# Two-layer mixer trunk on one core: the last output stage's final products five steps later, and the start of layer B reordered

## The chip, the core and the metric

The program runs on one core of a Trainium2 chip. The metric is the device time of one execution in microseconds (us); the number given for a kernel is the median over its runs. The engines are named as in the profile: PE (TensorE, the matrix products), DVE (VectorE), ACT (ScalarE), POOL (GpSimd) and SP (SyncE, which here only issues transfers). Each engine works through its own queue in order.

## The reference

The input x is 2048 positions by 1024 channels in float32. Two layers follow, each of the form x <- x + mixer(RMSNorm(x)), and then a last RMSNorm:

```
h = rmsnorm(x, norm_g[0]);  x = x + recurrent_mixer(h, ...)     # layer A
h = rmsnorm(x, norm_g[1]);  x = x + shortconv_mixer(h, ...)     # layer B
out = rmsnorm(x, final_g)
```

`rmsnorm` multiplies each position by the reciprocal root of the mean of its squares over the 1024 channels, and by a gain per channel. Layer A projects h to 2 x 1536 channels, runs a convolution, gates and a linear recurrence over the positions, and projects back to 1024. Layer B projects h to 4 x 1536 channels, forms products, a short convolution and a SiLU gate, and projects back.

## The kernel before

All tensors lie transposed, channels on the 128 partitions and positions along the row. The 2048 positions are four chunks `c` of 512, which form two halves of two chunks; 1024 channels are eight blocks `d` of 128. A float32 product is made of three float16 products (`mm3`, lines 500, 503 and 504): each operand is split into a high and a low float16 part, the high part by an ACT cast and the low part by a DVE subtraction (`add`, lines 311 and 313; weights in `split`, lines 420 and 421; the last stage's operands in `split_out`, lines 1117 and 1118).

The work has four stages: projection into layer A, projection out of A (`OutProj`, with `emitA` and `endA`), projection into B (`in_B`, made of units), projection out of B (`OutSums`, with `emitB`, `endB` and `last_chunk`). The two stages around the change are these.

**Layer B's beginning.** The products of B's projection use seven combinations of operand blocks in the manner of Strassen and Winograd. A unit is seven steps of 12 matmuls. `build_h` (line 329) makes the operands of h for one half: it normalises x blocks (`normed`, line 305, DVE), forms the sums and differences T1 to T4 (T1 at line 351, T3 at 367 and T4 at 371 on POOL; T2 at 357 on DVE), and splits B11, T1, T2, B21, B22, T3, T4 in this order, one of these groups of four per call. For the first half it runs beside the last products of A's output projection, in two parts (`besideA`, line 1603). For the second half it runs in `second_half` (line 1647), a side list that is advanced by one call after each product step of the units. There, chunk 2 is already normalised (`ready`), while the norm of chunk 3 has to wait for A's last output block: its squares are summed block by block into the tile `sa` (`add_square`, the addition on POOL, line 230), summed over the partitions by PE (`sums_of`, line 236, tile `ss`), and turned into `inv` by `inv_from` (line 244): root on ACT, reciprocal on DVE, four diagonal tiles `dg` on DVE (line 259), a PE product that spreads them (line 262, tile `pn`), a copy on ACT (line 265). `inv_between` (line 292) issues the two PE parts in two calls and places each behind the product that was last issued then (`pe_last`). The calls of the list are: first the four B11 splits, second the `ss` sums, third the inverse, fourth T1, and so on. An eviction of a product from its accumulator is at line 539 (DVE) or at 549 and 565 (ACT).

**Layer B's output projection.** `OutSums.run` makes seven products of four blocks `q` per half, again in combinations: a step is one accumulator of 18 matmuls. Each finished accumulator (`acc`, six buffers) is evicted by `add_to_x` (line 1428, DVE) one step after it was filled (`lag(1)`). After each step `tick` counts the deferred calls down. The final values of chunk 1 are complete with the sixth combination of the first half, those of chunk 0 four steps later, with the seventh. `endB` (line 1690) then defers the end of the chunk, a generator `ended`: for chunks 0 and 1 `inv_between` with POOL as queue sums by PE, takes the root and reciprocal, and issues two transfers from POOL: `r` to memory (line 252, `rd<-r`) and back, spread over the partitions (line 253, `inv<-rd`), the second waiting for the first. The next call multiplies the eight blocks by `inv` (line 1701, six on DVE, two on POOL) and stores them from SP (line 1702). The calls come four, five and six steps after the end of the chunk is reported; for chunk 2 they come after two, three and four. Chunk 3 ends in `last_chunk`.

The order of the instructions on each engine follows from the program's order, from priorities (evictions come first) and from the scheduler's own timing model, which is not the chip's.

Of the kernel before, what the change touches and what calls it, by code (L numbers as in the profile page):

```python
# [11 lines left out]
ALU = mybir.AluOpType  # L12
# [9 lines left out]
KB = D // P  # L22
# [24 lines left out]
def trunk(ctx, tc, xT, xn, prm, wa, ga, oa, wb, ob, out):  # L47
    nc = tc.nc
    v, s, g, sp = nc.vector, nc.scalar, nc.gpsimd, nc.sync
# [48 lines left out]
    def pair16(pool, tag, name, bufs):  # L98
        t = pool.tile([P, 2, ROW], F16, tag=tag, name=name, bufs=bufs)
        return t[:, :, 0:CH]  # L100
# [94 lines left out]
    def et(name, dt=F32):  # L195
        return buf(wk, "e", name, NE, dt)
# [16 lines left out]
    def xt(name, dt=F32):  # L213
        return buf(opp, "x", name, 36, dt)
# [10 lines left out]
    def add_square(acc, x, first, eng):  # L225
        if first:
            return s.activation(acc, x, AF.Square)
        sq = et("sq")[:, 0 : x.shape[1]]
        ins = s.activation(sq, x, AF.Square)
        squared[0] = eng.tensor_tensor(out=acc, in0=acc, in1=sq, op=ALU.add)  # L230
        return ins

    def sums_of(acc, ss, behind=None):

        for i in range(acc.shape[1] // P):
            ins = nc.tensor.matmul(  # L236
                ss[:, i : i + 1], acc[:, i * P : (i + 1) * P], ones[:, 0:1],
                start=True, stop=True,
            )
            if behind is not None:  # L240
                after(ins, behind)
        return ins

    def inv_from(ss, inv, queue, copy, behind=None):

        n = inv.shape[1] // P
        r = cst.tile([P, 4], F32, tag="r", name="r", bufs=2)[:, 0:n]
        s.activation(r, ss, AF.Sqrt, bias=epst[:, 0:1], scale=1.0 / D)
        v.reciprocal(r, r)
        if queue:  # L250
            rd = dr.tile([CH], F32, tag="rd", name="rd", bufs=2)
            queue.dma_start(rd.rearrange("(i p) -> p i", p=P), r)
            queue.dma_start(inv, rd.partition_broadcast(P))
            return
        pn = ps.tile([P, CH], F32, tag="g", name="pn", bufs=2)[:, 0 : n * P]
        dgs = buf(wk, "dg", "dg", 2)
        for i in range(n):
            dg = dgs[:, i * P : (i + 1) * P]
            v.tensor_scalar(
                out=dg, in0=col(PC_ID, P), scalar1=r[:, i : i + 1], scalar2=None, op0=ALU.mult  # L260
            )
            ins = nc.tensor.matmul(pn[:, i * P : (i + 1) * P], ones, dg, start=True, stop=True)  # L262
            if behind is not None:
                after(ins, behind)
        copy(inv, pn)
        return ins
# [25 lines left out]
    def inv_between(acc, inv, queue=None):  # L292

        ss = ps.tile([P, 4], F32, tag="g", name="ss", bufs=2)[:, 0 : acc.shape[1] // P]
        with tc.high_priority(PR):
            sums_of(acc, ss, pe_last[0])
        if not queue:
            yield
        with tc.high_priority(PR):
            inv_from(ss, inv, queue, s.copy, pe_last[0])  # L300
        yield


    def normed(l, x, kk, inv):
        return v.scalar_tensor_tensor(
            out=x, in0=x, scalar=gs[l][:, kk : kk + 1], in1=inv, op0=ALU.mult, op1=ALU.mult
        )

    def add(ops, name, k, src):
        t = pair16(opp, "op", "op", NOP)  # L310
        hi = s.activation(t[:, 0, :], src, AF.Copy)  # L311
        ops[name, k] = t
        return hi, v.tensor_tensor(out=t[:, 1, :], in0=src, in1=t[:, 0, :], op=ALU.subtract)  # L313
# [15 lines left out]
    def build_h(l, x, inv, ks, ops, ready=()):  # L329

        def norm(kk, c):
            if c not in ready:
                ins = normed(l, x[kk, c], kk, inv[c])
                if evac_last[0] is not None:
                    after(ins, evac_last[0])

        def block(name, k, kk, c):
            if (name, k) not in ops:  # L340
                norm(kk, c)
                add(ops, name, k, x[kk, c])

        t1, t2 = {}, {}
        for k in ks:
            block("B11", k, k, 0)
        yield
        for k in ks:
            norm(k, 1)
            t1[k] = et("t1")  # L350
            g.tensor_tensor(out=t1[k], in0=x[k, 1], in1=x[k, 0], op=ALU.subtract)
            add(ops, "T1", k, t1[k])
        yield
        for k in ks:
            norm(k + 4, 1)
            t2[k] = et("t2")
            v.tensor_tensor(out=t2[k], in0=x[k + 4, 1], in1=t1[k], op=ALU.subtract)
            add(ops, "T2", k, t2[k])
        yield
        for k in ks:  # L360
            block("B21", k, k + 4, 0)
        yield
        for k in ks:
            add(ops, "B22", k, x[k + 4, 1])
        yield
        for k in ks:
            g.tensor_tensor(out=x[k, 1], in0=x[k + 4, 1], in1=x[k, 1], op=ALU.subtract)
            add(ops, "T3", k, x[k, 1])
        yield
        for k in ks:  # L370
            g.tensor_tensor(out=t2[k], in0=x[k + 4, 0], in1=t2[k], op=ALU.subtract)
            add(ops, "T4", k, t2[k])
        yield

# [266 lines left out]
    def defer(fn, steps):  # L641
        deferred.append([steps, fn])
# [440 lines left out]
    def after(ins, first):  # L1083
        tc.add_manual_dep(
            ins.ins, first.ins.name,
            mybir.DependencyInfo(mybir.DependencyClass.NoSync, mybir.DependencyReason.SCHED_ONLY),
            reason="order",
        )
# [491 lines left out]
    hB, inv, sums, w0 = [{}, {}], {}, {}, {}  # L1580
    early, sws, xB, xh = [], [], {}, {}

    def emitA(c, d, xr, acc, undo):
        evac_last[0] = v.scalar_tensor_tensor(
            out=xr, in0=acc, scalar=undo, in1=xr, op0=ALU.mult, op1=ALU.add
        )
        sp.dma_start(x2[c][d * P : (d + 1) * P, :], xr)
        first = c not in sums
        if first:
            sums[c] = et("sa")  # L1590
            if c % 2 == 0:
                inv[c // 2] = [xt("inv") for i in range(2)]
        add_square(sums[c], xr, first, g)

    def endA(c):
        if c == 3:
# [41 lines left out]

    stay = [(d, c) for c in range(4) for d in range(KB) if c > 1]
    outA.run(emitA, endA, besideA, sideA, {dc: kept_x(*dc) for dc in stay})  # L1640
    x = {(d, c): xB[d, 2 + c] for d in range(KB) for c in range(2)}
    while early:
        run(early.pop(0))
    w0 = w0, ahead(1, wb[1], sws[1])
    acc3 = sums[3]

    def second_half():
        h = build_h(1, x, inv[1], range(4), hB[1], (0,))
        next(h)
        yield  # L1650
        yield from inv_between(acc3, inv[1][1])
        yield from h

    sideB = [second_half()]


# [33 lines left out]
    def endB(c, ts):  # L1690
        if ts is not CHUNK:
            defer(lambda: endings.append(last_chunk(c, ts)), 1 if ts is FIRST else 0)
            return
        iv = et("inv")

        def ended():
            yield from inv_between(sums[c], iv, g if c < 2 else None)
            for d in range(KB):
                f = kept[c, d]
                eng = g if d % 3 == 2 else v  # L1700
                eng.tensor_tensor(out=f, in0=f, in1=iv, op=ALU.mult)  # L1701
                sp.dma_start(out[d * P : (d + 1) * P, c * CH : (c + 1) * CH], f)

        steps = ended()
        for n in range(3):
            defer(lambda: next(steps, None), (4 if c < 2 else 2) + n)


    POOLED = (5, 7)
# [66 lines left out]

    ending = end_of_all()
    outB.run(emitB, endB, ending)
    tick(KB)
    while next(ending) != "idle":  # L1780
# [72 lines left out]
```

## Time and profile before

| | us |
|---|---|
| median of 3 runs | 2008.2 |
| lowest and highest run | 2005.45 and 2008.68 |
| the profiled execution's own time | 2011.81 |
| its span, first to last instruction | 2010.0 |
| PE busy | 1963.9 |
| DVE busy | 1259.9 |
| ACT busy | 1001.8 |
| POOL busy | 641.9 |

Busy time counts the stretches in which an engine has an instruction in work. The span lies 1.8 us below the time of the same execution. A number such as L1701 is a line of the kernel; `op<-t,op` reads "writes op, from t and op"; an arrow before a releaser says what ended the idle time.

### The profile page before, as it was taken

The numbers are of one execution on the slowest core, as the hardware profiler recorded it, in microseconds if no ns is written. First come the engines' busy times: TensorE is split into PE (matmuls) and PEld (weight loads), VectorE is DVE, ScalarE is ACT, GpSimd is POOL, SyncE is SP. The second block draws the span as 40 slices with busy tenths as digits, with TensorE's granted clock in tenths as the row PEclk, the third lists the DMA queues.
The fourth block names the chain that finished last, engine by engine and source line by source line (L and its number), as shares of the span: only waits on it lengthen the run. The fifth ranks groups of instructions, "written<-read, shape, count | busy, mean of one in ns | idle before, by whom it ended". The sixth has DMA issues, their size and how long they took to land. (4 is left out here: it accounts for less than half of the span.)

```text
span 2010.0 us, 25206 instructions
## 1 busy us (share of the span) xinstructions
PE 1963.9 (98%) x9064; PEld 916.0 (46%) x9064; DVE 1259.9 (63%) x2112; ACT 1001.8 (50%) x1816; POOL 641.9 (32%) x511
## 2 busy tenths in 40 slices
PE   8999999999999999998999999999999999999978
PEld 3444444444444444443444444444444444444436
DVE  7977666667574745479546757748547448654455
ACT  7878786868483623145443343343432432435332
POOL 0001010101010313365553583664644534512221
PEclk9999999999999999999999999999999999999989
DMA  9111313052104714421140251242220120595442
GB/s 311 49 63 50 102 38 113 24 168 83 65 17 157 248 66 162 95 79 63 63 152 32 79 163 43 95 142 79 74 100 22 53 90 21 194 378 200 134 152 85
DMA packets 130958, 216.25 MB, mean 108 GB/s; under 512 B 13200, under 2 KB 41488, under 8 KB 130832
## 3 DMA queue, kind: packets, MB, share of 16 engines
q1 hardware_dynamic: 130384, 213.58, 31.9%
q8 instruction: 71, 1.16, 0.3%
q0 software_dynamic: 448, 1.06, 0.2%
q14 instruction: 55, 0.45, 0.1%
HBM read 152.19 MB, written 62.40 MB: 107 GB/s over the span
## 5 line engine op out<-in xcount | busy, mean ns | idle before, releaser
L503 PEld LDWEIGHTS <-wc 128*128 128x128 f16 x2096 | 205.3, 98 | 271.1 <-issue 37.6
L500 PEld LDWEIGHTS <-wc 128*128 128x128 f16 x2096 | 207.9, 99 | 254.1 <-issue 19.6
L504 PEld LDWEIGHTS <-wc 128*128 128x128 f16 x2096 | 205.6, 98 | 257.3 <-issue 15.8
L503 PE MATMUL acc<-op,wc 128*128 128x512 f16 x752 | 285.3, 380 | 2.8 <-DVE op L313 2.8
L504 PE MATMUL acc<-op,wc 128*128 128x512 f16 x752 | 285.7, 380 | 0.0
L500 PE MATMUL acc<-op,wc 128*128 128x512 f16 x752 | 283.3, 380 | 1.3 <-ACT op L311 1.3
L903 POOL TENSOR_TENSOR u<-fixed,u 128x512 f32<-128x512 f32 x48 | 51.3, 1090 | 557.0 <-ACT fixed L900 557.0
L500 PE MATMUL q<-op,wc 128*128 128x512 f16 x576 | 217.4, 380 | 9.8 <-DVE pb L539 4.0
L503 PE MATMUL q<-op,wc 128*128 128x512 f16 x576 | 219.0, 380 | 0.0
L504 PE MATMUL q<-op,wc 128*128 128x512 f16 x576 | 218.5, 380 | 0.0
L421 DVE SCALAR_TENSOR_TENSOR wc<-ws,fixed,wc 128x512 f16<-128x512 f32 x104 | 104.4, 1008 | 90.5 <-ACT wc L420 81.0
L500 PE MATMUL p<-op,wc 128*128 128x512 f16 x384 | 146.1, 381 | 2.7 <-DVE pb L539 2.7
L500 PE MATMUL acc<-op,wf 128*128 128x512 f16 (+1 forms) x384 | 136.3, 355 | 11.1 <-DVE xo L1428 11.1
L503 PE MATMUL p<-op,wc 128*128 128x512 f16 x384 | 146.3, 381 | 0.0
L504 PE MATMUL p<-op,wc 128*128 128x512 f16 x384 | 146.2, 381 | 0.0
L500 PE MATMUL acc<-zs,wf 128*128 128x512 f16 x384 | 145.5, 379 | 0.0
L503 PE MATMUL acc<-zs,wf 128*128 128x512 f16 x384 | 145.5, 379 | 0.0
L504 PE MATMUL r<-op,wc 128*128 128x512 f16 x384 | 145.5, 379 | 0.0
L503 PE MATMUL r<-op,wc 128*128 128x512 f16 x384 | 145.5, 379 | 0.0
L500 PE MATMUL r<-op,wc 128*128 128x512 f16 x384 | 145.5, 379 | 0.0
L504 PE MATMUL acc<-zs,wf 128*128 128x512 f16 x384 | 145.2, 379 | 0.0
L504 PE MATMUL acc<-op,wf 128*128 128x512 f16 (+1 forms) x384 | 136.3, 355 | 0.0
(197 smaller groups left out, 3544.1 us busy)
## 6 DMA issues: line engine op xcount, KB each, us to landing
wr<-in_wb SPq DMA_DIRECT2D x104, 256.0 KB, 3.5
xs<-in_xT SPq DMA_DIRECT2D x48, 256.0 KB, 5.4
z<-sg SPq DMA_DIRECT2D x48, 256.0 KB, 2.0
zr<-z SPq DMA_DIRECT2D x48, 256.0 KB, 5.2
zr<-zT SPq DMA_DIRECT2D x48, 256.0 KB, 5.3
wr<-in_wa SPq DMA_DIRECT2D x44, 256.0 KB, 4.2
zB<-ed SPq DMA_DIRECT2D x36, 256.0 KB, 2.0
zT<-cg SPq DMA_DIRECT2D x36, 256.0 KB, 2.0
```

What stands on the lines that cost most here:

```text
L421: v.scalar_tensor_tensor(out=t[:, 1, :], in0=src, scalar=sw[:, 2:3], in1=t[:, 0, :], op0=ALU.mult, op1=ALU.subtract,)
L500: ins = nc.tensor.matmul(acc, wh, xh, start=start, stop=False, **kw)
L503: nc.tensor.matmul(acc, wh, xl, start=False, stop=False, **kw)
L504: return nc.tensor.matmul(acc, wl, xh, start=False, stop=stop, **kw)
L903: g.tensor_tensor(out=u, in0=w, in1=u, op=ALU.mult)
```

## The change

Three edits. First, T1, T3 and T4 in `build_h` (both halves) are computed by DVE rather than POOL, and so is the last addition of squares of layer A's output, that of block 7 of chunk 3. Second, `second_half` issues the `ss` sums in its first call, with the four B11 splits and now the four B21 splits as well; the inverse in its second call; T1 in its third. Third, for chunks 0 and 1 of the last stage the products with `inv` come nine steps after the report of the chunk's end, not five; the sums still come after four. Chunk 2 keeps its steps.

```diff
@@ build_h
-            g.tensor_tensor(out=t1[k], in0=x[k, 1], in1=x[k, 0], op=ALU.subtract)
+            v.tensor_tensor(out=t1[k], in0=x[k, 1], in1=x[k, 0], op=ALU.subtract)
...
-            g.tensor_tensor(out=x[k, 1], in0=x[k + 4, 1], in1=x[k, 1], op=ALU.subtract)
+            v.tensor_tensor(out=x[k, 1], in0=x[k + 4, 1], in1=x[k, 1], op=ALU.subtract)
...
-            g.tensor_tensor(out=t2[k], in0=x[k + 4, 0], in1=t2[k], op=ALU.subtract)
+            v.tensor_tensor(out=t2[k], in0=x[k + 4, 0], in1=t2[k], op=ALU.subtract)
@@ emitA
-        add_square(sums[c], xr, first, g)
+        add_square(sums[c], xr, first, v if (c, d) == (3, KB - 1) else g)
@@ second_half
         h = build_h(1, x, inv[1], range(4), hB[1], (0,))
+        steps = inv_between(acc3, inv[1][1])
+        next(steps)
         next(h)
-        yield
-        yield from inv_between(acc3, inv[1][1])
+        for k in range(4):
+            add(hB[1], "B21", k, x[k + 4, 0])
+        yield
+        next(steps)
+        yield
         yield from h
@@ endB
-        for n in range(3):
-            defer(lambda: next(steps, None), (4 if c < 2 else 2) + n)
+        for n in (4, 9) if c < 2 else (2, 3, 4):
+            defer(lambda: next(steps, None), n)
```

## Rows read from the trace of the kernel before

**Rows 1.** The page: span, and busy time of each engine.

```profile
span 2010.0 us, 25206 instructions
PE 1963.9 (98%) x9064; PEld 916.0 (46%) x9064; DVE 1259.9 (63%) x2112; ACT 1001.8 (50%) x1816; POOL 641.9 (32%) x511
```

**Rows 2.** Waits of PE, whole span: who and for what, us in total, times, longest.

```profile
PE acc L500 <- DVE xo L1428: 11.1, 1, 11.1
```

**Rows 3.** Waits of PE from 880 to 955 us.

```profile
PE q L500 <- DVE pb L539: 4.0, 2, 3.7
PE p L500 <- DVE pb L539: 2.7, 1, 2.7
PE q L500 <- DVE cg L539: 2.0, 1, 2.0
```

**Rows 4.** Timeline of DVE, last stage: start, us, instruction, idle before it, releaser.

```profile
1888.89 5.85 DVE L1701 TENSOR_TENSOR xo<-xo,inv 128x512 f32<-128x512 f32 x6 [7.72 <-DMA inv<-rd]
...
1916.32 5.83 DVE L1701 TENSOR_TENSOR xo<-xo,inv 128x512 f32<-128x512 f32 x6 [14.24 <-DMA inv<-rd]
```

**Rows 5.** Timeline of POOL, last stage: the two transfer pairs.

```profile
1874.30 0.80 POOL L252 DMA_DIRECT2D rd<-r  x1 [3.52 <-DVE r L249]
1884.36 0.55 POOL L253 DMA_DIRECT2D inv<-rd  x1 [9.27 <-PE acc L504]
...
1899.75 0.80 POOL L252 DMA_DIRECT2D rd<-r  x1 [7.37 <-DVE r L249]
1911.83 0.55 POOL L253 DMA_DIRECT2D inv<-rd  x1 [11.28 <-DMA rd<-r]
```

**Rows 6.** Timeline of PE, last stage: the sums of chunk 1 and of chunk 0.

```profile
1871.64 0.95 PE L236 MATMUL ss<-fixed,sa 128*128 128x1 f32 x8
...
1887.99 0.95 PE L236 MATMUL ss<-fixed,sa 128*128 128x1 f32 x8
```

**Rows 7.** Windows of PE: length, busy (matmuls), granted clock, DMA share, GB/s.

```profile
928.00:932.00 4.00, 4.00 (x11) 0.58 0.19 63
932.00:936.00 4.00, 4.00 (x20) 0.99 0.18 66
1923.53:1928.81 5.28, 5.28 (x13) 0.51 0.97 298
1928.81:1934.09 5.28, 5.28 (x27) 1.00 0.39 131
```

**Rows 8.** Timeline of SP, last stage: the eight stores of chunk 0.

```profile
1918.15 4.58 SPq L1702 DMA_DIRECT2D out_xT<-xo  x8
```

**Rows 9.** Windows, layer B's beginning: busy of PE, PEld, DVE, ACT, POOL; clock; DMA.

```profile
872.00:884.40 12.40, 12.40 (x67) 6.72 (x66) 5.29 (x11) 7.62 (x19) 2.34 (x2) 1.00 0.53 167
884.00:925.00 41.00, 35.58 (x157) 15.70 (x156) 40.58 (x44) 19.47 (x37) 30.57 (x19) 0.96 0.02 7
```

**Rows 10.** Groups of DVE and POOL, 884 to 925 us: busy, mean ns, idle before.

```profile
L313 DVE TENSOR_TENSOR op<-xs,op 128x512 f16<-128x512 f32 x12 | 12.4, 1075 | 0.0
L305 DVE SCALAR_TENSOR_TENSOR xs<-xs,fixed,inv 128x512 f32<-128x512 f32 x8 | 10.9, 1424 | 0.9 <-ACT inv L265 0.9
L371 POOL TENSOR_TENSOR t<-xs,t 128x512 f32<-128x512 f32 x4 | 8.5, 2168 | 1.2 <-DVE op L313 1.2
L367 POOL TENSOR_TENSOR xs<-xs 128x512 f32<-128x512 f32 x4 | 6.8, 1710 | 0.0
L351 POOL TENSOR_TENSOR t<-xs 128x512 f32<-128x512 f32 x4 | 6.7, 1704 | 11.0 <-DVE xs L305 11.0
```

**Rows 11.** Timeline of DVE while POOL is idle: four subtractions in one row.

```profile
907.89 2.48 DVE L313 TENSOR_TENSOR op<-t,op 128x512 f16<-128x512 f32 x4
```

**Rows 12.** Timeline of PE: the two parts of chunk 3's norm.

```profile
876.93 0.95 PE L236 MATMUL ss<-fixed,sa 128*128 128x1 f32 x8
...
882.71 1.05 PE L262 MATMUL pn<-dg,fixed 128*128 128x128 f32 x8
```

**Rows 13.** Waits of PE from 955 to 965 us.

```profile
PE q L500 <- DVE cg L539: 1.1, 1, 1.1
```

## The prediction

> **What bounds the kernel now.** The page comes first: PE is busy for 1963.9 of 2010.0 us [rows 1], so work taken off any other engine is worth nothing by itself, and only places where PE stands still, or runs at the lower clock, can give time back. Second, the waits of PE over the whole span: the longest single wait is 11.1 us, before a product of the last stage, for an eviction on DVE (L1428) [rows 2]. Third, the same view cut to the beginning of layer B: 8.7 us in four waits (4.0 + 2.7 + 2.0), all for evictions on DVE (L539) [rows 3]. Fourth, the windows with the granted clock. After the long wait the clock is at 0.51, the level of 1.2 GHz, and PE does 13 matmuls in 5.28 us where the next 5.28 us hold 27 [rows 7]; that costs 5.28 x 14/27 = 2.7 us. The same happens twice at B's beginning, after the two longest waits there; the pair of windows shown has 11 matmuls in 4.00 us against 20 [rows 7], so 9 x 0.20 = 1.8 us each, 3.6 us for both.
>
> The two places the change touches thus hold 11.1 + 2.7 = 13.8 us and 8.7 + 3.6 = 12.3 us, 26.1 us together, and this is the most that it can give there.
>
> **The products of chunks 0 and 1.** The DVE timeline shows why the last stage stalls. DVE works in order. It reached the products of chunk 1 (L1701) before `inv` had come and stood for 7.7 us; it did the same with those of chunk 0 and stood for 14.2 us [rows 4]. The evictions issued behind them stood too, and with six accumulators filled PE had to stop. `inv` is late because of its two transfers on POOL: from `rd<-r` to `inv<-rd` 10.1 and 12.1 us, from there to the product 4.5 us each time [rows 5, 4]. The sums of chunk 1 began at 1871.6 us [rows 6], the products at 1888.9: a chain of 17.3 us, where one step later is only (1888.0 - 1871.6 - 0.9)/4 = 3.9 us later [rows 6].
>
> The edit leaves the sums and moves the products from one step behind them to five, 5 x 3.9 = 19.5 us. For chunk 1 that covers the 17.3 us. For chunk 0 the sums start at 1888.0; its reciprocal, which stood behind chunk 1's products before, now stands ahead of them, so `rd<-r` goes out after 2.7 us (1874.3 - 1871.6 for chunk 1), and with the longer transfer `inv` comes at 1888.0 + 2.7 + 12.1 + 4.5 = 1907.3. The products come up on DVE behind the eviction of the fourth product after the sums, at about 1888.9 + 4 x 3.9 = 1904.5. DVE may wait 3 us; with six accumulators PE can go on for up to 6 x 3.9 = 23 us from there, and the products themselves are 5.8 us [rows 4]. So I take the whole 13.8 us. Bounds: 13.8 at most; nothing at least, if the scheduler's own order brings the products forward again.
>
> What moves with them: two products on POOL and eight stores on SP per chunk. On POOL the second transfer of chunk 0 waits up to 12.1 us for the first, and chunk 1's two products may now stand behind it, until about 1903. SP then stands at chunk 1's third store, with loads of later operands behind. Before, SP stood at the stores of chunk 0 until 1918.2 [rows 8] with such loads behind it as well, and the one wait of PE in that stage was for an eviction, not for an operand [rows 2]. I price this at nothing; the cover is the lead of the loads, and if it were gone PE would wait for an operand as long as POOL holds SP, up to 12.1 us. `inv` and the blocks keep their buffers four steps longer; this adds no instruction. The end of the kernel (chunks 2 and 3) is not touched.
>
> **Layer B's beginning.** From 884 to 925 us DVE is busy 40.58 of 41.00 us and POOL 30.57 [rows 9]. Together they slow each other: a subtraction takes 2.48/4 = 0.62 us with POOL idle [rows 11], but the twelve of one group take a mean of 1.07 us and the eight normalisations 1.42 us [rows 10]. Three terms relieve DVE:
>
> (a) POOL loses 8.5 + 6.8 + 6.7 = 22.0 us of T1, T3 and T4 [rows 10], 0.72 of its load here. The two DVE groups shown lose 12.4 - 12 x 0.62 = 5.0 us and about 10.9 - 8 x 0.7 = 5.3 us to the overlap (0.7 as my estimate for an unhindered normalisation, between 0.62 and the 0.74 of an eviction). 0.72 of 10.3 comes back, 7.4 us; the twelve subtractions put on DVE cost 12 x 0.62 = 7.4 us. By these groups alone DVE gains nothing and loses nothing; what smaller groups regain is on top.
>
> The Trainium skill (SBUF — State Buffer, section "Who interferes with whom") says that a DVE instruction with two SBUF inputs and a GpSimd instruction that reads SBUF exclude each other for a whole instruction, while one with a single SBUF input doesn't contend. The trace agrees in kind: the stretched groups read two SBUF tiles, and the 0.74 us evictions from PSUM are not stretched. By that rule alone term (a) would be 22.0 - 7.4 = 14.6 us of DVE time, not zero, and the time that of the fourth rival below.
>
> (b) The four B21 splits move from this stretch to before it: 4 x 1.07 = 4.3 us [rows 10]. There DVE is busy 5.29 of 12.40 us [rows 9], which is the cover; without it they would cost 2.5 us.
>
> (c) The sums stand at 876.9 us in PE's order, the spreading product at 882.7 [rows 12]. Each is now issued one call, that is one product of 12 matmuls, earlier: 12 x 0.20 = 2.4 us [rows 7] at least, and up to two products, 4.8 us, if PE's order closes up. The last addition of squares, on DVE instead of POOL, is on this chain and shortens it by under 1 us. I take 3.5 us.
>
> DVE is thus ahead by 0 + 4.3 + 3.5 = 7.8 us, against 8.7 us of waits. Waits as such don't fall one for one: I let each of the three lines [rows 3] keep 1.1 us, which is what such an eviction costs a little later, where POOL does less [rows 13], and which no fall of the clock followed. That leaves 3.3 us and takes 8.7 - 3.3 = 5.4 us and both clock losses, 3.6: **9.0 us**. Bounds: 12.3 us, and a loss of 7.4 us if the moved subtractions only lengthen DVE's queue ahead of the evictions. The twelve instructions moved in the first half's h lie beside A's output products, where PE waits for nothing; they cost nothing there, 7.4 us of DVE time without that cover.
>
> **Sum.** 13.8 + 9.0 = 22.8 us. Against the profiled execution's own 2011.8 us (span 2010.0) that is 1989.0; the median of the runs is 3.6 us lower, so as a median 2008.2 - 22.8 = **1985.4 us**.
>
> **Rivals.** *First, B's beginning stays as it is*: DVE pays for the moved subtractions what it regains. For it: term (a) by itself is zero, and all waits there are for DVE. Against: (b) and (c). Time: 2008.2 - 13.8 = 1994.4.
>
> *Second, half of the last stage's wait comes back elsewhere*: POOL's products of chunk 1 behind `inv<-rd` hold SP, and PE waits for an operand. For it: the 12.1 us transfer. Against: PE waited for no load while SP stood longer. Time: 2008.2 - 6.9 - 9.0 = 1992.3.
>
> *Third, slower*: VectorE's queue at B's beginning. If POOL's other work moves up into the freed time, so that each of the twelve subtractions takes as long as POOL's did (1.70 us [rows 10]), the queue grows by 12 x 1.70 = 20.4 us ahead of the evictions, and PE waits that long on top of its present waits. Time: 2008.2 - 13.8 + 20.4 = 2014.8. It makes the kernel slower from 13.8 us on. Against: only 30.57 - 22.0 = 8.6 us of other POOL work lie there.
>
> *Fourth, full exclusion*: each instruction of POOL on T1, T3 and T4 holds DVE up for its whole length, and DVE gets back all 22.0 us [rows 10] for 7.4. All waits at B's beginning go, with their clock losses. For it: DVE is never idle beside POOL and still falls behind [rows 9]. Against: by the two groups only 10.3 us are lost to all of POOL's work. Time: 2008.2 - 26.1 = 1982.1. It is the rule of the Trainium skill cited above.
>
> *Fifth, no change*: the scheduler orders by its own timing, puts the products back to where they were, and B's gain is lost too: 2008.
>
> **How the numbers follow.** Forecast 0.54, first rival 0.14, second 0.10, third 0.04, fourth 0.14, fifth 0.04. The forecast's own range is 1981 to 1991. Reaching to the first, second and fourth rival gives 1980 to 1996, which leaves out the third, the fifth and the tails. The low end is all 26.1 us with 2 us for small waits elsewhere. A measurement of this kernel can tell about 0.2%, 4.0 us, from no change: faster means below 2004.2, which the forecast and the first, second and fourth rival are: 0.92; same 0.04; slower 0.04.
>
> **What would show it.** Right: no wait of PE for L1428 over 2 us in the last stage and no window at half clock there; DVE's idle time before L1701 under 4 us; the products of the two chunks near 1891 and 1906 us, less the 9.0 us gained before them; PE's waits for L539 at B's beginning under 4 us; L305 and L313 near 0.7 us each. Wrong: a wait of PE for `op` or `wf` in the last stage, L1701 again with over 10 us of idle time before it, or waits for L539 at 8 us or more.

## The result, and the profile after

The changed kernel takes 1998.66 us as the median of 5 runs (1996.45 to 1999.18), the kernel before 2008.2 us as the median of 5 runs on the same chip (2005.45 to 2010.46). The ratio is 0.9947, with a 95% interval of 0.9936 to 0.9958: faster by 9.5 us. The prediction said 22.8 us faster and a range of 1980 to 1996; the measured time lies outside it. The profiled execution took 1997.66 us. One execution of the kernel before, beside the first four experiments, took 4221.7 us; the ratios leave it out.

The page's head and the waits of PE over the whole span answer to [rows 1, 2]:

```profile
span 1995.4 us, 25154 instructions
PE 1959.1 (98%) x9064; PEld 914.7 (46%) x9064; DVE 1257.5 (63%) x2137; ACT 1002.9 (50%) x1816; POOL 604.5 (30%) x486
```

```profile
PE acc L500 <- DVE xo L1428: 9.2, 1, 9.2
```

The first to look at is the second fence: the wait that was to go, 11.1 us before, is still there with 9.2 us. The line numbers behind 1650 have moved by five (L1701 is L1706 now).

**Layer B's beginning, after.** Waits of PE from 870 to 945 us, which answer to [rows 3]; the window of [rows 9] (busy of PE, PEld, DVE, ACT, POOL; clock; DMA); groups of DVE in it, to be read against [rows 10]; and the first product of layer B with the two PE parts of the norm, against [rows 12]:

```profile
PE q L500 <- DVE fixed L107: 1.0, 1, 1.0
PE q L500 <- DVE pb L539: 0.9, 1, 0.9
PE p L504 <- DVE wc L421: 0.8, 1, 0.8
```

```profile
884.00:925.00 41.00, 39.06 (x183) 17.60 (x181) 41.00 (x69) 17.96 (x33) 9.16 (x9) 1.00 0.06 20
```

```profile
L313 DVE TENSOR_TENSOR op<-xs,op 128x512 f16<-128x512 f32 x8 | 5.1, 673 | 0.0
L305 DVE SCALAR_TENSOR_TENSOR xs<-xs,fixed,inv 128x512 f32<-128x512 f32 x7 | 4.7, 740 | 0.0
...
L351 DVE TENSOR_TENSOR t<-xs 128x512 f32<-128x512 f32 x4 | 2.6, 677 | 0.0
```

```profile
868.85 0.38 PE L500 MATMUL p<-op,wc 128*128 128x512 f16 x1
...
875.32 0.95 PE L236 MATMUL ss<-fixed,sa 128*128 128x1 f32 x8
...
881.09 1.05 PE L262 MATMUL pn<-dg,fixed 128*128 128x128 f32 x8
```

The waits have fallen from 8.7 to 2.7 us, and the window's clock is 1.00, not 0.96. The second fall of before lay behind this window, at 928 us [rows 7]; in the changed kernel the clock is 1.00 there too, so both falls are gone. DVE is as busy as before, but gets 69 instructions done in the 41 us, not 44. A normalisation takes 0.74 us (1.42 before), a subtraction 0.67 us (1.07 before). POOL's busy time in the window is 9.2 us, not 30.6. The norm's parts stand 1.6 us earlier than in [rows 12], but so does nearly all of layer B in this execution. In the kernel before its first product began at

```profile
870.03 0.38 PE L500 MATMUL p<-op,wc 128*128 128x512 f16 x1
```

Measured from there, the sums came 6.9 us and the spreading product 12.7 us later; now it is 6.5 and 12.2 us. The norm has gained 0.4 us.

**The last stage, after.** The timeline of DVE with its idle times, which answers to [rows 4], and that of POOL, which answers to [rows 5]:

```profile
1861.82 0.17 DVE L249 RECIPROCAL r<-r 128x4 f32<-128x4 f32 x1
1864.52 0.75 DVE L1428 SCALAR_TENSOR_TENSOR xo<-acc,fixed,xo 128x512 f32<-128x512 f32 x1 [2.53 <-PE acc L504]
...
1868.40 0.75 DVE L1428 SCALAR_TENSOR_TENSOR xo<-acc,fixed,xo 128x512 f32<-128x512 f32 x1 [2.48 <-PE acc L504]
1876.20 4.04 DVE L1706 TENSOR_TENSOR xo<-xo,inv 128x512 f32<-128x512 f32 x3 [7.05 <-DMA inv<-rd]
...
1886.61 0.16 DVE L249 RECIPROCAL r<-r 128x4 f32<-128x4 f32 x1
1886.70 0.71 DVE L1428 SCALAR_TENSOR_TENSOR xo<-acc,fixed,xo 128x512 f32<-128x512 f32 x1
1887.33 0.73 DVE L1118 SCALAR_TENSOR_TENSOR op<-zr,fixed,op 128x512 f16<-128x512 f32 x1
1887.99 0.73 DVE L1428 SCALAR_TENSOR_TENSOR xo<-acc,fixed,xo 128x512 f32<-128x512 f32 x1
1888.65 0.73 DVE L1118 SCALAR_TENSOR_TENSOR op<-zr,fixed,op 128x512 f16<-128x512 f32 x1
1902.27 5.84 DVE L1706 TENSOR_TENSOR xo<-xo,inv 128x512 f32<-128x512 f32 x6 [12.88 <-DMA inv<-rd]
```

```profile
1862.28 0.80 POOL L252 DMA_DIRECT2D rd<-r  x1 [3.50 <-DVE r L249]
1871.66 0.55 POOL L253 DMA_DIRECT2D inv<-rd  x1 [8.58 <-DMA rd<-r]
...
1887.07 0.80 POOL L252 DMA_DIRECT2D rd<-r  x1 [7.36 <-DVE r L249]
1898.01 0.55 POOL L253 DMA_DIRECT2D inv<-rd  x1 [10.15 <-DMA rd<-r]
```

Count the evictions (L1428) between each reciprocal (L249) and its products (L1706): two for chunk 1, two for chunk 0. The same count stands in the kernel before, here for chunk 0, whose products follow at 1916.32 us [rows 4]:

```profile
1899.30 0.16 DVE L249 RECIPROCAL r<-r 128x4 f32<-128x4 f32 x1
1899.38 0.71 DVE L1428 SCALAR_TENSOR_TENSOR xo<-acc,fixed,xo 128x512 f32<-128x512 f32 x1
...
1900.68 0.73 DVE L1428 SCALAR_TENSOR_TENSOR xo<-acc,fixed,xo 128x512 f32<-128x512 f32 x1
```

The program issues the products four steps, that is four evictions, later, and on the engine they have not moved. Counted from PE's sums, the program had one eviction ahead of the products before and has five now; the engine has three in both kernels (for chunk 1 they begin at 1871.85, 1876.54 and 1880.42 us before, and at 1859.83, 1864.52 and 1868.40 us after). DVE still reaches them before `inv` is there, 7.05 and 12.88 us too early (7.72 and 14.24 in [rows 4]), and the difference to before is in the transfers: from `rd<-r` to `inv<-rd` 9.4 and 10.9 us, not 10.1 and 12.1. The windows of PE after the wait show the low clock as before (11 matmuls against 21 in 4.24 us, 2.0 us lost):

```profile
1909.48:1913.72 4.24, 4.24 (x11) 0.50 0.95 309
1913.72:1917.96 4.24, 4.24 (x21) 1.00 0.31 102
```

### The profile page after: what moved, and what is told of

It reads as the page before. It is cut to its first block, busy times and chain, and to the rows that moved or that the text cites. A ratio compares the mean times of both kernels' runs of the same rounds, so it can differ in the third digit from the quotient of the medians.

```text
span 1995.4 us, 25154 instructions
## 1 busy us (share of the span) xinstructions
PE 1959.1 (98%) x9064; PEld 914.7 (46%) x9064; DVE 1257.5 (63%) x2137; ACT 1002.9 (50%) x1816; POOL 604.5 (30%) x486
## 4 chain that ended last, share of the span: by engine, by line
PE 87%; DVE 6%; ACT 2%; DMA 2%; issue 2%; POOL 0%; SPq 0%; DVEq 0%; ACTq 0%; POOLq 0%
PE acc L500 14%; PE acc L503 14%; PE acc L504 14%; PE q L500 6%; PE q L504 6%; PE q L503 6%; PE p L504 4%; PE p L500 4%; PE p L503 4%; PE r L500 4%; PE r L504 4%; PE r L503 4%; PE pg L878 3%; DVE cg L1009 1%; DVE wc L421 1%
## 5 line engine op out<-in xcount | busy, mean ns | idle before, releaser
L421 DVE SCALAR_TENSOR_TENSOR wc<-ws,fixed,wc 128x512 f16<-128x512 f32 x104 | 101.3, 979 | 87.6 <-ACT wc L420 79.5
```

Of the source, the lines that this page charges most:

```text
L421: v.scalar_tensor_tensor(out=t[:, 1, :], in0=src, scalar=sw[:, 2:3], in1=t[:, 0, :], op0=ALU.mult, op1=ALU.subtract,)
```

## The experiments

Two theories stood at the start. Theory 1: the deferral changes the program's order only; the scheduler, which fills DVE by its own timing, puts the products where `inv` is ready by that timing. Theory 2: the deferral works, and what is left of the wait is something else (a slower transfer, DVE's load, or a wait that took the place of the old one). Each ratio is that of a kernel's runs to those of the kernel before on the same chip.

**The last stage's edit alone** on the kernel before:

```diff
-        for n in range(3):
-            defer(lambda: next(steps, None), (4 if c < 2 else 2) + n)
+        for n in (4, 9) if c < 2 else (2, 3, 4):
+            defer(lambda: next(steps, None), n)
```

> The kernel before with the last stage's edit alone (products with inv after nine steps, not five). Theory 1 (the deferral moves the products in the program, but the scheduler, which fills VectorE by its own timing, issues them where inv is ready by its timing, behind the same eviction as before): PE's wait for L1428 stays at 9 to 11 us, the time within 2 us of the kernel before. Theory 2 (the deferral does put the products off, and what is left of the wait after the change is a slower transfer): the products stand four evictions later on VectorE than before; the time is 2 to 3 us below the kernel before, and lower still with shorter transfers.

Measured: 2007.75 us, ratio 1.0004 (0.9995 to 1.0013). DVE's timeline around chunk 0's products:

```profile
1896.68 0.16 DVE L249 RECIPROCAL r<-r 128x4 f32<-128x4 f32 x1
1896.77 0.71 DVE L1428 SCALAR_TENSOR_TENSOR xo<-acc,fixed,xo 128x512 f32<-128x512 f32 x1
...
1898.07 0.74 DVE L1428 SCALAR_TENSOR_TENSOR xo<-acc,fixed,xo 128x512 f32<-128x512 f32 x1
...
1912.89 5.83 DVE L1701 TENSOR_TENSOR xo<-xo,inv 128x512 f32<-128x512 f32 x6 [13.42 <-DMA inv<-rd]
```

Again two evictions and a wait of 13.4 us; PE waits 9.6 us for L1428. The edit by itself is worth nothing that can be measured. Theory 2 falls. Of theory 1 the run shows that the products stay where they were; that the scheduler's timing has `inv` ready at this place is its guess at the reason, and no run shows it.

**Its counterpart**: the changed kernel with that edit undone (the same four lines, the other way round).

> The changed kernel with the last stage's edit undone: only layer B's beginning is changed. If all of the gain is from there (theory 1): 9 to 10 us below the kernel before, as the whole change, with PE's wait for L1428 at 9 to 11 us. If the last stage's edit gave the 2 us by which its wait fell in the two profiles (theory 2): 2 us above the changed kernel, about 2000.5.

Measured: 1998.13 us, ratio 0.9948 (0.9935 to 0.9961), the whole gain of the change; PE waits 9.9 us for L1428. So, as far as these intervals can tell, all of the change's gain comes from layer B's beginning.

**The order made binding**: the products are ordered behind the eviction that the program issued last.

```diff
@@ add_to_x
+                evac_last[0] = ins
                 if final:
@@ ended
-                eng.tensor_tensor(out=f, in0=f, in1=iv, op=ALU.mult)
+                ins = eng.tensor_tensor(out=f, in0=f, in1=iv, op=ALU.mult)
+                if c < 2:
+                    after(ins, evac_last[0])
```

> The changed kernel, with each product with inv of chunks 0 and 1 ordered behind the last eviction that the program has issued at that point, so that the nine steps hold on VectorE too. Theory 1 (VectorE stands at the products with the evictions behind it, and the deferral alone did not move them): PE's wait of 9.2 us and the 2.1 us at the lower clock after it go, 1998.7 - 11.3 = 1987.4; VectorE waits under 8 us before chunk 0's products. Rival (the wait only moves: POOL's transfer holds SP, later operands come late): PE waits for op or wf instead, and the time stays above 1994.

Measured: 1987.46 us, ratio 0.9903 (0.9889 to 0.9917). DVE's timeline from chunk 1's products (first line) to chunk 0's, and PE's waits in the last stage:

```profile
1879.18 5.85 DVE L1707 TENSOR_TENSOR xo<-xo,inv 128x512 f32<-128x512 f32 x6 [2.33 <-DMA inv<-rd]
...
1886.28 0.16 DVE L249 RECIPROCAL r<-r 128x4 f32<-128x4 f32 x1
1886.37 0.71 DVE L1428 SCALAR_TENSOR_TENSOR xo<-acc,fixed,xo 128x512 f32<-128x512 f32 x1
...
1887.66 0.74 DVE L1428 SCALAR_TENSOR_TENSOR xo<-acc,fixed,xo 128x512 f32<-128x512 f32 x1
...
1889.65 0.74 DVE L1428 SCALAR_TENSOR_TENSOR xo<-acc,fixed,xo 128x512 f32<-128x512 f32 x1
...
1892.44 0.75 DVE L1428 SCALAR_TENSOR_TENSOR xo<-acc,fixed,xo 128x512 f32<-128x512 f32 x1 [1.40 <-PE acc L504]
1901.61 5.85 DVE L1707 TENSOR_TENSOR xo<-xo,inv 128x512 f32<-128x512 f32 x6 [8.42 <-DMA inv<-rd]
...
1908.71 0.74 DVE L1428 SCALAR_TENSOR_TENSOR xo<-acc,fixed,xo 128x512 f32<-128x512 f32 x1
```

```profile
PE acc L500 <- DVE xo L1428: 1.6, 1, 1.6
```

Four evictions now stand between, and DVE still waits 8.4 us, a little over the 8 us expected. One cause is in the first two lines: the reciprocal of chunk 0 still stands behind the products of chunk 1, though PE began chunk 0's sums at 1875.90 us and ACT the root at 1877.34. So `rd<-r` goes out at 1886.74, 10.8 us after the sums. But DVE has caught up with PE by then (the last eviction before the products waits for PE itself), and PE stands for 1.6 us only, at full clock. No wait for `op` or `wf` takes the old wait's place. The last rows also show how long PE can go on: it stops 15.5 us, four steps, after the eviction at 1892.44, not six. A11, S2, S3 and A22 of a half add into the same four accumulators, so a step needs the eviction of the step four before it.

**No transfers**: for chunks 0 and 1 the inverse is spread by PE, with chunk 2's steps.

```diff
-            yield from inv_between(sums[c], iv, g if c < 2 else None)
+            yield from inv_between(sums[c], iv)
...
-        for n in (4, 9) if c < 2 else (2, 3, 4):
+        for n in (2, 3, 4):
```

> The changed kernel with no transfers for the inverse of chunks 0 and 1: it is spread by PE as for chunk 2, with chunk 2's steps. Theory 1: VectorE no longer waits before L1706, PE's wait for L1428 goes, and PE gains two spreading products of about 0.8 us each: 1998.7 - 11.3 + 1.6 = 1989. Rival (the wait comes from VectorE's load of products, 5.8 us for each chunk, not from the transfers): a wait of PE for L1428 of several us stays, the time is above 1994.

Measured: 1986.6 us, ratio 0.9896 (0.9882 to 0.9910), below the expected 1989. PE has no wait for L1428, and DVE waits 1.5 us in all before the products of these two chunks:

```profile
DVE xo L1706 <- ACT inv L265: 1.5, 1, 1.5
```

The twelve products are still on DVE, and they are now issued four steps after the report, not five as before the change. So it was the transfers that held it and not its load.

**The binding order without the deferral**: the pinned kernel with the products back at five steps.

```diff
-        for n in (4, 9) if c < 2 else (2, 3, 4):
-            defer(lambda: next(steps, None), n)
+        for n in range(3):
+            defer(lambda: next(steps, None), (4 if c < 2 else 2) + n)
```

> The pinned kernel with the products back at five steps: the order behind the last issued eviction alone. Theory 1 (what counts is how many evictions stand between a chunk's reciprocal and its products on VectorE; the pin at five steps leaves two, as in the changed kernel): 1998 to 1999 with PE's wait for L1428 at 9 to 11 us. Rival (the ordering itself, at whatever step, repairs the stage): 1988 to 1991.

Measured: 1998.05 us, ratio 0.9947 (0.9933 to 0.9960); two evictions, a wait of DVE of 13.0 us and one of PE of 9.2 us. At five steps the pin asks for one eviction between the sums and the products, and the scheduler already puts three there, so it binds nothing. Neither half of the remedy shortens the time measurably alone; together they give about 11 us (10.7 us between 1987.46 us and the run without the deferral on the same chip).

**Layer B's beginning, the order alone**: only `second_half` changed, POOL keeps T1, T3, T4 and the last addition of squares.

```diff
@@ second_half
+        steps = inv_between(acc3, inv[1][1])
+        next(steps)
         next(h)
-        yield
-        yield from inv_between(acc3, inv[1][1])
+        for k in range(4):
+            add(hB[1], "B21", k, x[k + 4, 0])
+        yield
+        next(steps)
+        yield
```

> The kernel before with the second edit alone: the sums, the four B21 splits and the inverse come a call earlier, while T1, T3, T4 and the last addition of squares stay on POOL. Theory A (prediction's terms b and c: 7.8 us of VectorE's time come from the order, nothing from the engine): PE's waits for L539 at layer B's beginning fall from 8.7 us to under 4 us and both falls of the clock go, about 1999. Theory B (POOL's instructions hold VectorE up, and that is what is left behind the evictions): the waits stay at 5 us or more, the time is at 2003 or above.

Measured: 2010.73 us, ratio 1.0014 (1.0005 to 1.0022): no gain, rather a loss of 1 to 4 us. Waits of PE from 870 to 960 us and the window:

```profile
PE q L500 <- DVE pb L539: 6.4, 2, 3.8
PE p L500 <- DVE pb L539: 2.7, 1, 2.7
PE q L500 <- DVE cg L539: 2.1, 1, 2.1
```

```profile
884.00:925.00 41.00, 32.42 (x143) 14.26 (x141) 41.00 (x46) 15.43 (x30) 31.29 (x20) 0.94 0.08 26
```

With POOL busy for 31.3 of 41.0 us DVE gets 46 instructions done, and the waits are 11.2 us, not 8.7. Of the edit's two parts one has reached the engines: DVE has eight, not twelve, splits of x blocks (`op<-xs,op` at L313, [rows 10]) in the window. The other has not:

```profile
868.55 0.38 PE L500 MATMUL p<-op,wc 128*128 128x512 f16 x1
...
875.46 0.95 PE L236 MATMUL ss<-fixed,sa 128*128 128x1 f32 x8
...
881.23 1.05 PE L262 MATMUL pn<-dg,fixed 128*128 128x128 f32 x8
```

The sums and the spreading product stand 6.9 and 12.7 us behind layer B's first product, as before. Issued a call earlier in the program, they have kept their place on PE. Theory A of this run falls; what the run tests is the earlier splits, and not an earlier norm.

**The engines alone**: T1, T3, T4 and the last addition of squares on DVE, calls in the order of before.

```diff
-            g.tensor_tensor(out=t1[k], in0=x[k, 1], in1=x[k, 0], op=ALU.subtract)
+            v.tensor_tensor(out=t1[k], in0=x[k, 1], in1=x[k, 0], op=ALU.subtract)
...
-        add_square(sums[c], xr, first, g)
+        add_square(sums[c], xr, first, v if (c, d) == (3, KB - 1) else g)
```

> The kernel before with the first edit alone: T1, T3, T4 and the last addition of squares on VectorE, the order of the calls as before. Theory A (prediction's term a is zero): waits for L539 stay near 8.7 us, the time within 2 us of the kernel before. Theory B (full exclusion: VectorE gets 22.0 us back for 7.4): L305 falls to 0.7 us each, the waits fall under 4 us with both falls of the clock, about 1999.

Measured: 2000.94 us, ratio 0.9960 (0.9946 to 0.9973). Waits of PE from 870 to 960 us and the group of normalisations:

```profile
PE p L500 <- ACT wc L420: 2.1, 1, 2.1
PE q L500 <- DVE pb L539: 1.1, 2, 0.6
```

```profile
L305 DVE SCALAR_TENSOR_TENSOR xs<-xs,fixed,inv 128x512 f32<-128x512 f32 x8 | 5.4, 743 | 0.4 <-ACT inv L265 0.4
```

The waits for L539 are 1.1 us, L305 takes 0.74 us. The engines alone give 8 us of the 9.5. Theory B holds for the waits and for L305. Of the two falls of the clock one is left: behind the wait of 2.1 us for ACT (first line) PE does 12 matmuls in the 4 us from 928 us, at a clock of 0.66, and 18 in the next 4 us, where 4 us at full clock hold 20; that is 2.0 us. Whether the order adds something on top (2 us between this median and that of the run without the deferral) isn't settled: the intervals, 0.9946 to 0.9973 and 0.9935 to 0.9961, overlap. From layer B's first product to the end, the one profiled execution of each took 1129.8 us with the engines alone, 1126.9 without the deferral and 1140.0 before, which speaks for an addition.

**The first half's h back on POOL**, the rest as changed (`build_h` takes the engine as an argument, `g` for the first half).

> The changed kernel with T1, T3 and T4 of the first half's h back on POOL; those of the second half stay on VectorE. The prediction priced the twelve moved instructions of the first half at nothing: within 1.5 us of the changed kernel, 1998.7. Rival (the freed POOL time beside the last output products of layer A is part of the gain): 2 us or more above it.

Measured: 1994.42 us, ratio 0.9930 (0.9916 to 0.9943), which by the expectation would have been a cost of those twelve instructions, on the other side from the rival. So it was repeated beside the changed kernel on one chip:

> The changed kernel once more, beside the next three on the same chip. Both theories: 0.994 to 0.996 of the kernel before, near 1998.5.

> T1, T3 and T4 of the first half's h on POOL once more. If the 4 us by which it lay below the changed kernel are the beginning of the execution, which differs from run to run by that much with the same code: within 1.5 us of the changed kernel on this chip. If moving the first half's twelve instructions to VectorE costs time (VectorE is fuller beside the last output products of layer A): 2 to 4 us below it.

Measured: 1998.05 us for the changed kernel (0.9952, 0.9939 to 0.9964) and 1997.44 us for the first half on POOL (0.9949, 0.9936 to 0.9961). The difference of 4 us did not come again, and the same code gave 1994.42 and 1997.44 us. So no cost of the twelve instructions is shown, which is what they were priced at.

**Together**, with the first half on POOL:

> The pinned kernel with the first half's h on POOL. If the two add up: about 11 us below the changed kernel from the pin, and as much again as the first half gives alone on this chip, so 1984 to 1988; PE's wait for L1428 under 2 us.

> The inverse of chunks 0 and 1 spread by PE, and the first half's h on POOL. If the two add up: 1983 to 1987, no wait of PE for L1428, the fastest of all kernels here.

Measured: 1985.43 us with the binding order (0.9889, 0.9874 to 0.9904) and 1986.59 us with PE's spreading (0.9897, 0.9883 to 0.9910); PE has no wait for L1428 in either. Which of the two is better can't be told here; both beat the changed kernel by over 11 us. The expectation that the second would be the fastest didn't come true.

## Why the prediction was wrong, step by step

**The products of chunks 0 and 1: 13.8 us forecast, none measured.** This is the step that failed, and it failed in one sentence: "The products come up on DVE behind the eviction of the fourth product after the sums". That reads the order on the engine out of the order in the program. The front part of this document says that the order on an engine also follows from the scheduler's own timing, and the trace of before could have been asked: there, too, the products do not stand where the program issues them, behind one eviction after the sums, but behind three. In the changed kernel it is three again, where the program has five. The prediction named this case, as its lower bound of nothing for this stage and as its fifth rival, but tied the rival to a loss at layer B as well and gave it 0.04. It should have stood beside the forecast for this stage alone.

Where the order did bind, PE's wait fell to 1.6 us and the time to 1987.46 us, so moving the products behind the evictions does what the prediction said of it. But a second step fails there too: the reciprocal of chunk 0, "which stood behind chunk 1's products before, now stands ahead of them". It stands behind them in every run with the transfers, the pinned ones too. So in the pinned run `rd<-r` went out 10.8 us after the sums, not 2.7, and DVE waited 8.4 us, not 3.

**The tolerance of the wait.** That "with six accumulators PE can go on for up to 6 x 3.9 = 23 us" was wrong as well: it is four steps, 15.5 us. It didn't decide here, but with the order binding it leaves 1.6 us of wait in one execution and none in another.

**The size of the wait.** The 13.8 us were read from one execution whose transfer for chunk 0 took 12.1 us. In the nine other executions whose products stood three evictions behind the sums, PE's wait was 8.4 to 9.9 us, and three of these had the last stage's code of before (9.9 us without the deferral, 8.9 us with the order alone, 9.9 us with the engines alone). The profiled execution of before, 2011.81 us, lay above all five of its timed runs, 1.4 us above the highest.

**Layer B's beginning: 9.0 us forecast, 9.6 us measured** (1998.13 against 2007.69 us, the run without the deferral). That the sizes meet is luck; the working was not right. Term (a), the engines, was put at zero, and is nearly all of the gain: 8 us alone. Term (c), 3.5 us for an earlier norm, did not come about: behind layer B's first product the norm gained nothing by the order alone and 0.4 us by the engines alone, where the sums stand 6.5 and the spreading product 12.2 us behind it, as in the changed kernel. This is the same mistake as in the last stage, an earlier place in the program taken for one on the engine. Term (b), the four B21 splits, did leave the window, and gave no time alone. Why it gave none is not shown; what the run does show is POOL as busy as before (31.3 us) and PE's waits no shorter. The terms were added as if DVE's time were worth the same wherever it is saved, and that is not what this run shows.

Term (a) was mis-sized by taking two groups and 0.72 of their loss. By the groups with two SBUF inputs together: L305, L313, L357 and L421 took 38.4 us for 36 instructions before (the two L313 groups, 12 and 10, with 12.4 and 8.0 us; L357 3.6 us for four; L421 3.5 us for two) and would have taken 24.1 us at the prices of the run with the engines alone, so 14.3 us came back for the 8.0 us that the twelve subtractions cost there. The price of 0.62 us "with POOL idle" is not quite that: in [rows 11] POOL's L371 began at 908.65 us, 0.8 us into the row of 2.48 us. The run with the engines alone has 0.66 us for the same subtraction.

The Trainium skill's rule that was weighed (SBUF — State Buffer, section "Who interferes with whom": a DVE instruction with two SBUF inputs and a GpSimd instruction that reads SBUF exclude each other) is borne out in kind: in the run with the engines alone L305, L313 and L357, which read two SBUF tiles, fall to 0.68 to 0.74 us, and the evictions from PSUM (L539) were 0.74 us with and without. Full exclusion of 22.0 us, as the fourth rival had it, is more than the 14.3 us found; the waits went nearly as far as that rival said, though.

**What was priced at nothing** held: the first half's twelve instructions, the stores on SP and the products on POOL behind `inv<-rd` (no wait of PE for an operand in the last stage in any run).

**The third rival**, VectorE's longer queue, didn't come about: POOL's other work in the window was 8.6 us before and is 9.2 us after, and the moved subtractions took 0.67 us each.

## What to carry to other kernels

Where a scheduler orders each engine by a timing of its own, a later or earlier place in the program need not move anything: here the products stood three evictions behind the sums whether the program had one or five, and the norm kept its place on PE. Give the order itself, and count in the trace what stands between a wait's cause and the waiting instruction, before and after. A wait for a transfer costs what is queued behind the waiting instruction, so either bind the queue's order or take the transfer away. And when DVE falls behind, look first at whether POOL reads SBUF beside it: twelve instructions moved onto the busier engine let that engine finish more in the same time, and four splits put ahead of the crowded stretch did not shorten a wait.

## What the runs showed of the hardware

The transfer `rd<-r`, 2 KB from 128 partitions to memory, took 9.0 to 12.1 us from its issue to that of the transfer that waits for it, for chunks 0 and 1 of the last stage over all runs that have it. Among the runs whose products stood three evictions behind the sums, the longest for chunk 0, 12.1 us, went with PE's longest wait, 11.1 us, and the shortest, 10.2 us, with the shortest wait, 8.4 us. The same matmuls took twice the time for some 4 to 5 us after a wait of 9 to 11 us in the last stage; a fall of the clock also followed the wait of 3.7 us at layer B's beginning [rows 7] and the one of 2.1 us in the run with the engines alone, and none the one of 1.6 us in the pinned run. Beside a busy POOL, DVE got less done: in the same 41 us it finished 44 to 46 instructions with POOL busy for over 30 us, and 69 with POOL busy for 9.2 us or 13.5 us, though the mix of instructions is not quite the same.
